# Turning B and x of a state-space layer by 32x32 blocks and DMAs instead of by TensorE transposes

## The chip, the cores and the metric

The kernel runs on one core of a Trainium2 chip. The metric is device time in microseconds (us) for one execution. TensorE (PE in the profile) does the matmuls, with its weight loads shown as PEld; VectorE is DVE, ScalarE is ACT, GpSimd is POOL; SyncE (SP) only issues DMAs here.

## The reference, cut to what matters

Two layers on 512 tokens of width 1024, with a residual around each: a state-space layer (a chunked scan) and a latent attention layer, then a final RMS norm. The change lies in the first layer, whose scan is, for one of 8 groups of 4 heads (64 wide), with the sequence cut in 4 chunks of 128 tokens:

```python
cb = einsum('bctgn,bcsgn->bgcts', cc, bc)                       # C B^T within a chunk
y_diag = einsum('bgcts,bgrcts,bcsgrp->bctgrp', cb, decay_in, xc)  # xc = x * dt
chunk_states = einsum('bctgn,bgrct,bctgrp->bcgrpn', bc, decay_to_end, xc)
y_off = einsum('bctgn,bcgrpn,bgrct->bctgrp', cc, entering, exp(a_cum))
y = y_diag + y_off + d_skip * xs                                # then gate, group norm, out projection
```

B, C, x and the gate z come out of one input projection of the layer, a convolution over 4 tokens and a SiLU.

## The kernel before

Activations lie transposed: 128 channels on the partitions, 512 tokens along the free axis. A projection is done in about fp32 precision with three fast matmuls per 128x128 block of weights: the weight and the input are each split into a high and a low part (`whi`, `wlo`, `ah`, `al`), by a ScalarE copy (L272) and a VectorE subtraction (L273). Each output block of 128 channels takes 24 matmuls of 512 columns (8 input blocks times 3, L291), in four lots of 6.

A loop over the 8 groups interleaves two things on TensorE. The feed is the input projection of the next group, `ssm_in(g + 1)`: six blocks B, C, x0, x1, z0, z1 of 24 matmuls, so 144 in all. The pieces are the steps of the scan of the present group, class `SSD`: `cb` (turn B with 3 transposes into PSUM, L71, copy it to `BT` by ScalarE, L73; 8 small matmuls C B^T, L77; mask it and multiply it into the four decay tiles L, L79 and L81), `x(0)` and `x(1)` (turn a pair of heads with 4 transposes, L89, then multiply by dt into `xdt`, L92, and by the decay to the chunk's end into `xw`, L94), `states` (3 matmuls of `BT` and `xw`, issued as 6, L105, and the scan over chunks, L109 to L113) and `y` (matmuls L130 and L138, then VectorE L144 to L148).

`sched` sets the order on TensorE by hand: each lot of 6 matmuls of the feed adds 1.296 to a counter, and a piece is put in when its due time is reached. The due times of groups 1 to 7 are `P1`: `cb` 1.0, `x(0)` 2.4, `x(1)` 3.8, `states` 12.0, `y` 18.2; so `cb` comes after 1 lot of the next projection, `x(0)` after 2, `x(1)` after 3, `states` after 10 and `y` after 15 of 24. The group norm of the group before (`GN`, 16.84) comes after 13 lots. In the last group the feed is the output projection instead, and its own group norm is due at `G7` = 33.0, after 26 lots. `mla` follows.

Only TensorE's order is written out. On the other engines and on the DMA queues the framework's scheduler places an instruction when its inputs are ready and nothing that stands earlier in the program wants the engine; each engine and queue then works through its list in that order.

SyncE's queue issues nearly all DMAs: the weights (`load_weight`, L263, two buffers `raw` of 128x1024 fp32), the decay rows `L` (L627, once the `yd` matmuls of the group before have freed their buffers) and the rows `E` (L123, L124). The last step of the first layer already turns a tensor by way of DRAM, once, for the residual: VectorE turns 32x32 blocks (L681), and four DMAs per tile write them to `hd` (L684) in runs of 32 values.

Of the kernel before, what the change touches and what calls it, by code (L numbers as in the profile page):

```python
# [10 lines left out]
F32 = mybir.dt.float32  # L11
# [4 lines left out]
P = 128  # L16
T = 512
D = 1024
KD = D // P
NCH = T // P  # L20
# [17 lines left out]
SU = (0.64, 1.42)  # L38
P0 = (6.0, 6.8, 11.91, 15.25, 17.25, 24.88, 34.5)
P1 = (1.0, 2.4, 3.8, 12.0, 18.2)  # L40
GN = 16.84
G7 = 33.0
SF = (0.02, 0.1, 2.1, 3.1)
# [11 lines left out]
class SSD:  # L55
# [8 lines left out]
    def cb(self):  # L64
        nc, net, wk, v = self.nc, self.net, self.wk, self.nc.vector
        B, C = self.st["B"], self.st["C"]
        ch = lambda ap: ap.rearrange("p (c s) -> p c s", c=NCH)
        pb = net.ssd_aux()
        for c in range(3):
            s = slice(c * P, (c + 1) * P)  # L70
            nc.tensor.transpose(pb[:, s], B[:, s], net.ident)  # L71
        self.BT = wk.tile([P, 3 * P], F32, tag="BT", name=net.nm("BT"), bufs=1)
        nc.scalar.copy(self.BT[:], pb[:, :3 * P])  # L73
        pc = net.ssd_aux()
        for c in range(NCH):
            s = slice(c * P, (c + 1) * P)
            nc.tensor.matmul(pc[:, s], B[:, s], C[:, s], start=True, stop=True)  # L77
        cb = wk.tile([P, T], F32, tag="cb", name=net.nm("cb"), bufs=2)
        v.tensor_tensor(ch(cb[:]), ch(pc[:]), net.triu[:, None, :].to_broadcast([P, NCH, P]), op=ALU.mult)  # L79
        for L in self.L:  # L80
            v.tensor_tensor(L[:], L[:], cb[:], op=ALU.mult)  # L81

    def x(self, j):
        nc, net, wk, v = self.nc, self.net, self.wk, self.nc.vector
        x = self.st[f"x{j}"]
        px = net.ssd_aux()
        for c in range(NCH):
            s = slice(c * P, (c + 1) * P)
            nc.tensor.transpose(px[:, s], x[:, s], net.ident)  # L89
        h0 = 4 * self.g + 2 * j  # L90
        xp = wk.tile([P, NCH, 2, 64], F32, tag="xdt", name=net.nm("xdt"), bufs=2)
        v.tensor_tensor(xp[:], px[:].rearrange("p (c h d) -> p c h d", c=NCH, h=2),  # L92
                        self.dt[:, :, h0:h0 + 2].unsqueeze(3).to_broadcast([P, NCH, 2, 64]), op=ALU.mult)
        v.tensor_tensor(self.xw[:, :, 2 * j:2 * j + 2, :], xp[:, :3],  # L94
                        self.dend[:, :3, h0:h0 + 2].unsqueeze(3).to_broadcast([P, 3, 2, 64]), op=ALU.mult)
        self.xdt.append(xp)
# [55 lines left out]
class Net:  # L152
# [8 lines left out]
    def build(self):  # L161
        tc, nc, ctx = self.tc, self.nc, self.ctx
        pool = lambda name, bufs, **k: ctx.enter_context(tc.tile_pool(name=name, bufs=bufs, **k))
        self.const = pool("const", 1)
        self.wraw = pool("wraw", 2)
        self.whi = pool("whi", 3)
        self.wlo = pool("wlo", 3)
        self.act = pool("act", 8)
        self.o16 = pool("o16", 16)
        self.nrm = pool("nrm", 1)  # L170
        self.res = pool("res", 8)
        self.dram = pool("dram", 1, space=bass.MemoryType.DRAM)

        const = self.const
        self.xs = []
        self.cols = const.tile([P, C_N], F32, name="cols")
        self.ident = const.tile([P, P], F32, name="ident")[:]
        self.rows = const.tile([P, 2 * NH], F32, name="rows")

        self.phase, self.group, self.before, self.head = "", [], [], None  # L180
        self.wq = []
        self.wpos = self.wload = 0
        self.wraws = []
        self.wready = {}
        for g in range(NG):
            for i in range(6):
                self.wq.append(("w", U_IN + 6 * g + i))
        for i in range(16):
            self.wq.append(("w", U_OUT0 + i))
        for i in range(6):  # L190
            self.wq.append(("w", U_M1 + i))
        self.wq += [("w", U_MZ + i) for i in range(3)] + [("ua", 0), ("w", U_MZ + 3), ("ub", 0), ("uc", 0), ("w", U_MZ + 4)]
        out = [("w", U_OUT1 + i) for i in range(16)]
        for h in range(14):
            j = h // 2 + 1
            self.wq += [("ua", j)] if h % 2 == 0 else [("ub", j), ("uc", j)]
            if h < 11:
                self.wq.append(("w", U_MZ + 5 + h))
            self.wq += [out.pop(0) for _ in range({11: 1, 12: 1, 13: 2}.get(h, 0))]
        self.wq += out  # L200

        with tc.tile_pool(name="ps_s", bufs=1, space=bass.MemoryType.PSUM) as ps, \
                tc.tile_pool(name="ssm", bufs=2) as wk:
            self.ps, self.wk = ps, wk
            self.ssm()
        with tc.tile_pool(name="ps_m", bufs=1, space=bass.MemoryType.PSUM, reuse_waits="tile") as ps, \
                tc.tile_pool(name="mla", bufs=2, reuse_waits="tile") as wk:
            self.ps, self.wk = ps, wk
            self.mla()
# [50 lines left out]
    def load_weight(self, kind, idx):  # L260
        n = {"w": 1024, "ua": 1024, "ub": 640, "uc": 512}[kind]
        raw = self.wraw.tile([P, n], F32, tag="raw", name=self.nm("raw"))
        self.nc.sync.dma_start(raw[:], self.t[kind][idx])  # L263
        return raw

    def split_weight(self, raw, cuts=()):
# [70 lines left out]
    def sumsq(self, tiles, n, pstag, pool=None, tags=("r0", "rt", "rr"), after=None):  # L337
        nc = self.nc
        acc = None
        for x in tiles:  # L340
            sq = self.nrm.tile([P, T], F32, tag="sq", name=self.nm("sq"), bufs=SQ)
            i = nc.scalar.activation(sq[:], x, AF.Square)
            if after is not None:
                self.link(i, [after])
            if acc is None:
                acc = self.nrm.tile([P, T], F32, tag="sqa", name=self.nm("sqa"))
                nc.vector.tensor_scalar(acc[:], sq[:], self.eps_of(n), None, op0=ALU.add)
            else:
                nc.vector.tensor_tensor(acc[:], acc[:], sq[:], op=ALU.add)
        pool = pool or self.nrm  # L350
        hi = pool.tile([P, T], F32R, tag=tags[0], name=self.nm("sqh"))
        lo = pool.tile([P, T], F32R, tag=tags[1], name=self.nm("sql"))
        nc.scalar.copy(hi[:], acc[:])
        nc.vector.tensor_tensor(lo[:], acc[:], hi[:].bitcast(F32), op=ALU.subtract)
        ps = self.ps.tile([P, T], F32, tag=pstag, name=self.nm("pssq"), bufs=self.bufs[pstag])
        nc.tensor.matmul(ps[:], self.onesr[:], hi[:], start=True, stop=False)
        nc.tensor.matmul(ps[:], self.onesr[:], lo[:], start=False, stop=True)
        return ps[:]

    def ssm(self):  # L360
        tc, nc, t, wk = self.tc, self.nc, self.t, self.wk
# [12 lines left out]
        for k in range(KD):  # L374
            x = self.res.tile([P, T], F32, tag="res", name=self.nm("x"))
            nc.sync.dma_start(x[:], t["x"][k])
            self.xs.append(x)
            if k % 2 == 0:
                s = slice(k * P, (k + 2) * P)
# [15 lines left out]
        for k in range(KD):  # L395
            a = self.o16.tile([P, T], F32R, tag="o", name=self.nm("vh"))
# [32 lines left out]
            ul.append(b)  # L429

        gn = []
        self.silus(0)
        for g in range(NG):
            ys, q = [], []
            pieces = [] if g == 0 else [(GN, late)]
            if g == 0:
                begin = lambda: q.append(SSD(self, 0, self.lexp(0), ys))
                pieces += [(SU[0] + SU[1] * k, scaled) for k in range(KD)]
                pieces += [(P0[0], step), (P0[1], step), (P0[1] + 0.1, begin)]
                at = P0[2:]  # L440
            else:
                q.append(SSD(self, g, self.lexp(g), ys))
                at = P1
            pieces += [(at[0], lambda: q[0].cb()), (at[1], lambda: q[0].x(0)), (at[2], lambda: q[0].x(1)),
                       (at[3], lambda: q[0].states()), (at[4], lambda: q[0].y())]
            if g + 1 < NG:
                mid = (vh, vl, lambda: r, MID) if g == 0 else (uh, ul, None, 0)
                self.sched(self.ssm_in(g + 1, uh, ul, mid), pieces)
                self.silus(g + 1)
                late = functools.partial(lambda g, ys: gn.extend(self.gnorm(g, ys)), g, ys)  # L450
            else:
                self.part = []
                pieces.append((G7, lambda: gn.extend(self.gnorm(g, ys))))
                self.sched(self.out_half(gn, 0, U_OUT0, [t["x"][k] for k in range(KD)]), pieces)
# [616 lines left out]
```

## Time and profile before

| | us |
|---|---|
| median of 3 runs (lowest to highest) | 837.02 (836.73 to 837.34) |
| the profiled execution | 836.13 |
| its span in the trace | 834.0 |

The difference of 2.1 us between the last two lies outside the span, at start and end. In the trace, the scan layer's groups 1 to 6 follow each other with one period: the matmuls after `yd` begin at 197.55, 237.67, 277.79 us and so on. The first layer ends at about 415 us. A row of the chain of waits gives the start, the length and the work that the end of the kernel waited for; in that chain a matmul counts from one start to the next, so 60 matmuls of 512 columns take 13.83 us, while the groups of instructions give each a longer, overlapping time.

### The profile page before, as it was taken

How to read it: one execution, taken by the hardware profiler on the slowest of the kernel's cores; microseconds unless marked ns; L12 is line 12 of the kernel's file. 1: busy time of each engine (PE TensorE's matmuls, PEld its weight loads, DVE VectorE, ACT ScalarE, POOL GpSimd, SP SyncE). 2: the span in 40 equal slices, each digit the busy share in tenths (PEclk: the TensorE clock that was granted, in tenths of full speed). 3: DMA queues.
4: the chain of work that ended last, by engine and by line, in shares of the span. 5: the costliest groups of instructions: out<-in, count | busy, mean ns of one | idle time of the engine just before them, and what ended most of it. 6: DMA issues, size and time to landing. Idle time of an engine off the chain costs nothing.

```text
span 834.0 us, 11549 instructions
## 1 busy us (share of the span) xinstructions
PE 819.3 (98%) x4228; PEld 691.8 (83%) x4228; DVE 644.9 (77%) x1234; ACT 450.4 (54%) x794; POOL 0.2 (0%) x4
## 2 busy tenths in 40 slices
PE   7999999999999999999999999999999999999996
PEld 5887888888888888888888888888888888888885
DVE  7999898979787989778566787786767869675544
ACT  7567755545465657434353654556547557554233
POOL 0000000000000000000000000000000000000000
PEclk9999999999999999999999999999999999999999
DMA  6364543423242423333555142222222224331212
GB/s 227 103 191 141 155 147 106 152 99 129 101 139 90 152 76 127 115 121 94 130 130 132 54 130 64 79 72 76 63 64 58 90 78 152 101 97 56 86 66 101
DMA packets 50856, 90.55 MB, mean 109 GB/s; under 512 B 21552, under 2 KB 23088, under 8 KB 50800
## 3 DMA queue, kind: packets, MB, share of 16 engines
q1 hardware_dynamic: 50080, 88.77, 34.0%
q10 hardware_dynamic: 720, 1.05, 0.3%
q8 instruction: 33, 0.54, 0.3%
q14 instruction: 23, 0.19, 0.1%
HBM read 83.12 MB, written 4.33 MB: 105 GB/s over the span
## 4 chain that ended last, share of the span: by engine, by line
PE 92%; DVE 3%; DMA 2%; ACT 1%; SPq 1%; issue 0%; DVEq 0%; ACTq 0%
PE mm L291 55%; PE ot L941 11%; PE s L793 5%; PE mm L300 4%; PE po L835 4%; PE mm L773 3%; PE pt L817 2%; PE yd L138 2%; PE yd L291 1%; PE aux L130 1%; PE aux L105 1%; DMA x<-in_x_dram 1%; PE aux L77 1%; PE aux L89 1%; DMA L<-ac_d 1%; DVE wlo L273 1%
## 5 line engine op out<-in xcount | busy, mean ns | idle before, releaser
L272 ACT CAST whi<-raw 128x1024 fp32r<-128x1024 f32 (+3 forms) x132 | 127.0, 965 | 210.3 <-PE mm L291 172.8
L273 DVE TENSOR_TENSOR wlo<-raw,whi 128x1024 fp32r<-128x1024 f32 (+3 forms) x132 | 146.8, 1115 | 54.6 <-ACT whi L272 54.3
L291 PE MATMUL mm<-ah,whi 128*128 128x512 f32 x384 | 154.0, 401 | 0.0
L291 PE MATMUL mm<-ah,wlo 128*128 128x512 f32 x384 | 150.3, 391 | 0.4 <-DVE wlo L273 0.4
L291 PE MATMUL mm<-al,whi 128*128 128x512 f32 x384 | 149.9, 390 | 0.0
L291 PE MATMUL mm<-vh,whi 128*128 128x512 f32 x224 | 89.4, 399 | 0.8 <-ACT whi L272 0.8
L291 PE MATMUL mm<-vh,wlo 128*128 128x512 f32 x224 | 87.9, 392 | 0.7 <-DVE wlo L273 0.7
L291 PE MATMUL mm<-vl,whi 128*128 128x512 f32 x224 | 87.6, 391 | 0.0
L291 PEld LDWEIGHTS mm<-ah,wlo 128*128 128x128 f32 x384 | 72.1, 188 | 16.1 <-DVE wlo L273 0.8
L291 PEld LDWEIGHTS mm<-ah,whi 128*128 128x128 f32 x384 | 72.2, 188 | 15.3 <-issue 1.4
L291 PEld LDWEIGHTS mm<-al,whi 128*128 128x128 f32 x384 | 72.2, 188 | 14.4 <-DVE al L312 0.3
L941 PE MATMUL ot<-whi,ah 128*128 128x512 f32 (+1 forms) x136 | 52.4, 385 | 0.0
L941 PE MATMUL ot<-whi,al 128*128 128x512 f32 (+1 forms) x136 | 51.5, 379 | 0.0
L941 PE MATMUL ot<-wlo,ah 128*128 128x512 f32 (+1 forms) x136 | 51.4, 378 | 0.0
L291 PEld LDWEIGHTS mm<-vh,wlo 128*128 128x128 f32 x224 | 42.1, 188 | 10.7 <-DVE wlo L273 1.5
L291 PEld LDWEIGHTS mm<-vh,whi 128*128 128x128 f32 x224 | 42.2, 188 | 9.4 <-ACT whi L272 1.1
L223 ACT ACTIVATE p<-p,st 128x128 f32<-128x128 f32 (+1 forms) x64 | 36.1, 564 | 25.3 <-DVE st L805 25.2
L291 PEld LDWEIGHTS mm<-vl,whi 128*128 128x128 f32 x224 | 42.2, 188 | 7.3
L821 ACT CAST ph<-pt 128x512 fp32r<-128x512 f32 (+1 forms) x64 | 26.4, 421 | 33.3 <-PE pt L817 32.8
L291 PE MATMUL mm<-ch,whi 128*128 128x512 f32 x104 | 42.6, 410 | 0.0
L291 PE MATMUL mm<-ch,wlo 128*128 128x512 f32 x104 | 40.9, 393 | 0.0
L291 PE MATMUL mm<-cl,whi 128*128 128x512 f32 x104 | 40.8, 392 | 0.0
(223 smaller groups left out, 1637.7 us busy)
## 6 DMA issues: line engine op xcount, KB each, us to landing
raw<-in_w_dram SPq DMA_DIRECT2D x100, 512.0 KB, 3.3
L<-ac_d SPq DMA_DIRECT2D x32, 256.0 KB, 3.9
E<-ea_d SPq DMA_DIRECT2D x32, 128.0 KB, 3.5
raw<-in_ua_dram SPq DMA_DIRECT2D x8, 512.0 KB, 3.3
raw<-in_ub_dram SPq DMA_DIRECT2D x8, 320.0 KB, 2.8
x<-in_x_dram SPq DMA_DIRECT2D x8, 256.0 KB, 4.4
res<-in_x_dram SPq DMA_DIRECT2D x8, 256.0 KB, 3.1
hd<-ht SPq DMA_DIRECT2D x32, 64.0 KB, 3.5
```

The source lines that it names most:

```text
L138: nc.tensor.matmul(yd[64 * h:64 * h + 64, s], self.xdt[j][:, c, h, :], self.L[2 * j + h][:, s], start=True, stop=True)
L223: i = self.nc.scalar.activation(out, in_, func, **k)
L272: nc.scalar.copy(hi[:, a:b], raw[:, a:b])
L273: nc.vector.tensor_tensor(lo[:, a:b], raw[:, a:b], hi[:, a:b].bitcast(F32), op=ALU.subtract)
L291: self.nc.tensor.matmul(ps, a, b, start=i == 0, stop=i == len(seq) - 1)
L300: self.nc.tensor.matmul(p, seq[i][0], seq[i][1], start=i == 0, stop=i == 3 * ks - 1)
L773: nc.tensor.matmul(ps[:, c2 * 256:(c2 + 1) * 256], a, b, start=i == 0, stop=i == 5)
L793: nc.tensor.matmul(ps[:, :n], x[:, s], y[:, :n], start=k == 0, stop=k == 4)
L817: nc.tensor.transpose(pt[:, (b - kb) * P:(b - kb + 1) * P], probs[h][b][:, kb * P:(kb + 1) * P], self.ident)
L821: nc.scalar.copy(ph[:, :n], pt[:, :n])
L835: nc.tensor.matmul(po[:, kb * P:], x, y, start=kb == 0 and k == 0, stop=kb == NCH - 1 and k == 2)
L941: nc.tensor.matmul(ps[:, a:b], x, y, start=start and i == 0, stop=stop and i == 5)
```

## The change

For groups 2 to 7 (`FLIP = 2`) the 3 transposes of B and the 8 of x leave TensorE. In their place stand two new pieces. `flip` turns x0, x1 and B by VectorE in 32x32 blocks into tiles `tp`, and writes each with 4 DMAs of 64 KB into one of two DRAM tensors, so that the turned tensor lies there by rows. `back` reads x0 and x1 (256 KB each, runs of 512 bytes) into the `xdt` tiles and B (192 KB) into `BT`. `x(j)` then multiplies the loaded tile by dt in place. The due times of these groups are `P2`: `flip` 0.2, `cb` 1.0, `back` 8.0, `x(0)` 11.5, `x(1)` 11.6, `states` 15.5, `y` 21.0. From group 0's pieces on, all weights of both layers go over GpSimd's queue instead of SyncE's.

```diff
+P2 = (0.2, 1.0, 8.0, 11.5, 11.6, 15.5, 21.0)
+FLIP = 2
...
     def cb(self):
...
-        pb = net.ssd_aux()
-        for c in range(3):
-            s = slice(c * P, (c + 1) * P)
-            nc.tensor.transpose(pb[:, s], B[:, s], net.ident)
-        self.BT = wk.tile([P, 3 * P], F32, tag="BT", name=net.nm("BT"), bufs=1)
-        nc.scalar.copy(self.BT[:], pb[:, :3 * P])
+        if self.g < FLIP:
+            pb = net.ssd_aux()
+            for c in range(3):
+                s = slice(c * P, (c + 1) * P)
+                nc.tensor.transpose(pb[:, s], B[:, s], net.ident)
+            self.BT = wk.tile([P, 3 * P], F32, tag="BT", name=net.nm("BT"), bufs=1)
+            nc.scalar.copy(self.BT[:], pb[:, :3 * P])
...
+    def flip(self):
+        nc, net, wk = self.nc, self.net, self.wk
+        d = net.flip_d[self.g % 2]
+        turned = d[:].rearrange("(j a) n -> a j n", a=32)
+        for m, name in enumerate(("x0", "x1", "B")):
+            t = wk.tile([P, T], F32, tag="u", name=net.nm("tp"), bufs=3)
+            nc.vector.transpose(t[:], self.st[name][:])
+            for i in range(4):
+                n = m * P + 32 * i
+                nc.sync.dma_start(turned[:, :, n:n + 32], t[32 * i:32 * i + 32, :].rearrange("a (j n) -> a j n", n=32))
+
+    def back(self):
+        nc, net, wk = self.nc, self.net, self.wk
+        rows = net.flip_d[self.g % 2][:].rearrange("(c p) n -> p c n", p=P)
+        self.px = []
+        for j in range(2):
+            xp = wk.tile([P, NCH, 2, 64], F32, tag="xdt", name=net.nm("xdt"), bufs=2)
+            nc.sync.dma_start(xp[:].rearrange("p c h d -> p c (h d)"), rows[:, :, j * P:(j + 1) * P])
+            self.px.append(xp)
+        self.BT = wk.tile([P, 3 * P], F32, tag="BT", name=net.nm("BT"), bufs=1)
+        nc.sync.dma_start(self.BT[:].rearrange("p (c n) -> p c n", c=3), rows[:, :3, 2 * P:])
...
     def x(self, j):
...
+        if self.g < FLIP:
+            px = net.ssd_aux()
+            for c in range(NCH):
+                s = slice(c * P, (c + 1) * P)
+                nc.tensor.transpose(px[:, s], x[:, s], net.ident)
+            px = px[:].rearrange("p (c h d) -> p c h d", c=NCH, h=2)
+            xp = wk.tile([P, NCH, 2, 64], F32, tag="xdt", name=net.nm("xdt"), bufs=2)
+        else:
+            xp = self.px[j]
+            px = xp[:]
+        v.tensor_tensor(xp[:], px,
                         self.dt[:, :, h0:h0 + 2].unsqueeze(3).to_broadcast([P, NCH, 2, 64]), op=ALU.mult)
...
     def load_weight(self, kind, idx):
...
-        self.nc.sync.dma_start(raw[:], self.t[kind][idx])
+        self.wqueue.dma_start(raw[:], self.t[kind][idx])
...
+        self.flip_d = [self.dram.tile([T, 3 * P], F32, name=f"flip{i}") for i in range(2)]
...
-                at = P1
+                at = P1 if g < FLIP else (P2[1],) + P2[3:]
+                if g >= FLIP:
+                    pieces += [(P2[0], lambda: q[0].flip()), (P2[2], lambda: q[0].back())]
...
+            self.wqueue = nc.gpsimd
```

More of the change, by code (lines that the diff above doesn't have):

```diff
@@ L85, in x @@
         x = self.st[f"x{j}"]
[L86 to L89, printed above, removed]
         h0 = 4 * self.g + 2 * j
-        xp = wk.tile([P, NCH, 2, 64], F32, tag="xdt", name=net.nm("xdt"), bufs=2)
-        v.tensor_tensor(xp[:], px[:].rearrange("p (c h d) -> p c h d", c=NCH, h=2),
+        if self.g < FLIP:
[9 more added lines that the diff above has]
+        v.tensor_tensor(xp[:], px,
                         self.dt[:, :, h0:h0 + 2].unsqueeze(3).to_broadcast([P, NCH, 2, 64]), op=ALU.mult)
@@ L180, in build @@
         self.phase, self.group, self.before, self.head = "", [], [], None
+        self.wqueue = nc.sync
         self.wq = []
```

## The prediction

> **What bounds the kernel now.** I read first the head of the page with the chain of waits by engine, then the busy time by stretch, then the chain through one group.
>
> ```profile
> span 834.0 us, 11549 instructions
> PE 819.3 (98%) x4228; PEld 691.8 (83%) x4228; DVE 644.9 (77%) x1234; ACT 450.4 (54%) x794; POOL 0.2 (0%) x4
> PE 92%; DVE 3%; DMA 2%; ACT 1%; SPq 1%; issue 0%; DVEq 0%; ACTq 0%
> ```
>
> ```profile
> core 0: us, PE busy (x) PEld busy (x) DVE busy (x) ACT busy (x) POOL busy (x), PEclk, DMA share, GB/s
> 197.55:209.18 11.63, 11.63 (x52) 9.61 (x53) 11.60 (x26) 6.52 (x12) 0.00 (x0) 1.00 0.56 184
> 197.55:237.67 40.12, 40.12 (x216) 33.67 (x216) 34.16 (x61) 22.32 (x34) 0.00 (x0) 1.00 0.35 118
> 97.00:137.20 40.20, 40.20 (x217) 33.76 (x216) 38.98 (x73) 26.61 (x43) 0.00 (x0) 1.00 0.41 128
> 52.00:97.00 45.00, 44.00 (x248) 36.57 (x248) 39.74 (x66) 32.99 (x61) 0.00 (x0) 1.00 0.60 186
> ```
>
> TensorE sets the end. From 197.55 to 237.67 us (one group) it is busy for all of 40.12 us at full granted clock, so what leaves its list there shortens the group, if nothing that it needs comes late. VectorE is second: 34.16 of 40.12 us, 85%, and without a gap in the first 11.6 us. The chain through that group:
>
> ```profile
> 197.55 13.83 PE mm L291 x60
> 211.38 0.33 PE aux L71 x3
> 211.71 0.89 PE aux L77 x8
> 212.60 1.39 PE mm L291 x6
> 214.00 0.43 PE aux L89 x4
> 214.43 1.39 PE mm L291 x6
> 215.82 0.44 PE aux L89 x4
> 216.26 9.56 PE mm L291 x42
> 225.82 1.30 PE aux L105 x6
> 234.43 1.34 PE aux L130 x12
> 235.77 1.90 PE yd L138 x32
> 237.67 2.50 PE mm L291 x10
> ```
>
> The whole chain is TensorE's, and the eleven transposes (L71, L89) are links of it.
>
> **What leaves TensorE.** In the chain they take 0.33 + 0.43 + 0.44 = 1.20 us. Each x piece also cuts the feed: a lot of 6 matmuls between pieces takes 1.39 us, against 6 x 9.56/42 = 1.37 in the long run, so two cuts less give some 0.05. That is 1.25 us a group, and 6 x 1.25 = **7.5 us**. The BT copy (L73) leaves ScalarE, which has 22.32 of 40.12 us to do and so gives no time back.
>
> [...]
>
> **What VectorE gets.**
>
> ```profile
> L681 DVE STREAM_TRANSPOSE ht<-res x8: 699/711/712, 388.2 to 431.6; 128x512 f32<-128x512 f32 x8
> L684 SPq DMA_DIRECT2D hd<-ht x32: 341/487/856, 389.0 to 448.9; - x32
> DMA to landing us min/median/max: 2.3/3.4/3.8
> L92 DVE TENSOR_TENSOR xdt<-aux,dt 128x512 f32<-128x512 f32 x16 | 10.3, 684 | 0.0
> L94 DVE TENSOR_TENSOR xw<-xdt,dec 128x384 f32<-128x384 f32 x16 | 8.3, 551 | 0.0
> ```
>
> The first two rows are this same step in another place (times in ns as min/median/max). Three transposes of 0.711 us add 2.13 us a group. L92 reads SBUF in place of PSUM; L94 has two SBUF inputs already, 0.551 us for 384 columns or 1.43 ns a column, where L92 has 0.684 for 512, 1.34 ns, so I leave it at 0.684. VectorE then has 34.16 + 2.13 = 36.3 us in a group of 38.9, or 93%. What hides this is that VectorE is not in the chain; the stretch from 97.00 shows how far that goes: VectorE at 38.98 of 40.20 us, 97%, and TensorE still busy throughout. So nothing for it.
>
> **The way of x through DRAM.** It has a deadline, and this is where the change is decided. I count from T0, the end of the `yd` matmuls of the group before (197.55 us in the chain above).
>
> The deadline: `states` now comes after 12 lots in place of 10. From T0 there are 42 matmuls left of the old feed (`y` sits after 17 lots, 102 of 144), 6 of the new one, 0.89 us of L77, then 66 more. At 13.83/60 = 0.2305 us each, 114 matmuls are 26.3, so T0 + 27.2.
>
> When x1 is ready: before, its 24th matmul is the 6th after T0. Now `y` comes two lots later, so it lies 6 matmuls ahead of `y`: 1.39 + 1.34 + 1.90 = 4.63 us before T0, a shift of 6.0 us.
>
> ```profile
> 205.82 0.64 ACT L232 ACTIVATE x<-x 128x512 f32<-128x512 f32 x1
> ...
> 209.83 1.05 ACT L272 CAST whi<-raw 128x1024 fp32r<-128x1024 f32 x1 [2.86 <-PE mm L291]
> ```
>
> ```profile
> 202.04 1.22 DVE L273 TENSOR_TENSOR wlo<-raw,whi 128x1024 fp32r<-128x1024 f32 x1
> ...
> 204.68 2.24 DVE L634 TENSOR_SCALAR L<-L,ac 128x128 f32<-128x128 f32 x11
> ...
> 208.49 0.69 DVE L349 TENSOR_TENSOR sqa<-sqa,sq 128x512 f32<-128x512 f32 x1
> ```
>
> Its SiLU ended at 206.46, T0 + 8.9, so now near T0 + 2.9. The first gap of VectorE came at 209.18, T0 + 11.6.
>
> No row shows this round trip, so I bound it. The reads' nearest rows are those of `hr` and, slower, of `L`; `raw` serves for the weights further on:
>
> ```profile
> hr<-hd SPq DMA_DIRECT2D x8, 256.0 KB, 2.9
> L<-ac_d SPq DMA_DIRECT2D x32, 256.0 KB, 3.9
> raw<-in_w_dram SPq DMA_DIRECT2D x100, 512.0 KB, 3.3
> ...
> L923 SPq DMA_DIRECT2D hr<-hd x8: 319/320/332, 691.5 to 704.1; - x8
> ```
>
> - Early end: transpose done at T0 + 3.6; 4 issues of 0.49 us, landing 3.4 later, T0 + 9.0; three reads issued in 1.0 and landed 2.9 later, T0 + 12.9; L92 and L94 for both pairs 2 x (0.68 + 0.55) = 2.5, so T0 + 15.4. That is 11.8 us early.
> - Late end: all three transposes wait for the gap, T0 + 13.7; 4 issues of 0.86 and a landing of 3.8, T0 + 20.9; reads 1.0 + 3.9, T0 + 25.8; VectorE 2.5, T0 + 28.3. That is 1.1 us too late in each group.
>
> So the stall is 0 at the one end and 6 x 1.1 = 6.6 us at the other; below nothing it cannot be. I take 0: the middle, T0 + 21.8, is 5.4 us early, and in VectorE's first 11.6 us other work of the next feed (L273, L634 above) is already taken in between the steps of `y`, so a transpose can be too. x0 and B are ready earlier than x1.
>
> **SyncE's queue.** It gets 12 x 0.49 + 3 x 0.32 = 6.8 us of issues a group and loses six weights. Behind a `back` that waits for the last write stand only `L` and `E` rows, for `y` at the end of the group (their buffers come free after T0 in both versions); with the weights gone nothing that TensorE needs sooner is held up. If the weights had stayed, they would stand behind that wait.
>
> **Weights on GpSimd's queue.** No DMA in this trace comes from there. The nearest row is SyncE's: landing after 3.3 us at the median. How much later may they be? The buffer freed by the subtraction at 202.04 (ended 203.26) is used by the ScalarE copy at 209.83: 6.6 us. That copy waits for TensorE to release a `whi` (its row says so); three lie in turn, so its own first matmul is 48 matmuls, some 11 us, later, 2.3 of which go to copy and subtraction. The cover is 6.6 - 3.3 + 8.7 = 12 us a weight; if it were gone, each further us of delay would cost one on TensorE per weight. Both bounds (as fast, or twice 3.3) give nothing. A gain is bounded by the idle time of TensorE while groups 0 and 1 start, when weights do queue behind other issues: 45.00 - 44.00 = 1.0 us. I take 0.
>
> [...]
>
> **The end of the layer.** `y` of group 7 moves two lots nearer to its group norm.
>
> ```profile
> 356.30 1.90 PE yd L138 x32
> 365.87 0.68 DVE L354 TENSOR_TENSOR sql<-sqa,sqh 128x512 fp32r<-128x512 f32 x1
> 373.39 0.23 PE pssq L356
> ```
>
> Before, the norm's inputs were ready at 366.55, 8.4 us after `yd`; TensorE asks for them after 9 lots now, 54 x 0.23 = 12.4 us. Covered.
>
> **Sum.** 836.13 - 7.5 = 828.6 us for the profiled execution. That execution lies 0.9 us under the median of 837.02, so the forecast is **829.5 us**.
>
> **Rivals.**
>
> 1. *Nearly hidden or nearly lost: the late end above.* TensorE waits at `states` for `xw` some 1.1 us a group: 829.5 + 6.6 = 836.1. For it: VectorE's full 11.6 us after T0. Against: x1's shift of 6.0 us. About no change.
>
> 2. *The round trip becomes the bound.* VectorE keeps the transposes behind its backlog and all 12 writes queue behind them: T0 + 13.7; twelve issues of about 0.6 us (between the median 0.49 and the longest 0.86) are 7.2; landing 3.8, T0 + 24.7; reads 1.0 + 3.9, VectorE 2.5, T0 + 32.1. That is 4.9 us late, 29.4 over six groups: 859 us. It is slower from the point where the wait exceeds 1.25 us a group. For it: SyncE issues one DMA after another, and VectorE, in order, may stand at L92 with a weight's subtraction behind it. Against: x0 and B need not wait for x1, and 8 of 12 issues can go first.
>
> [...]
>
> **How the numbers follow.** Forecast (no stall beyond 0.3 us a group, 828 to 831.5): 0.62. Part of the gain eaten, 831.5 to 835.3: 0.07. Rival 1: 0.09. Rival 2: 0.19, half of it under 840 since its wait can be anything past its point. Rival 3: 0.03. The measurement can tell about 0.2%, 1.7 us, from no change, so faster is 0.62 + 0.07 less a remainder = 0.68, same 0.10, slower 0.22. The forecast's own range is 828 to 831.5; the lower end takes 1.0 us of start-up gain and half a us for the run. To leave out no more than 2 in 10 the upper end goes to 840.
>
> **What would show it.** Right: the period between `yd` ends falls from 40.12 to about 38.9 us in six groups; L71 counts 6 and L89 16; VectorE near 93% there; no wait at L105. Wrong: TensorE waiting at L105 for L94, or L94's line behind a DMA of `xdt` (rivals 1 and 2); ScalarE's L272 behind `raw` and TensorE behind L272 (rival 3); or a period that shrinks by less with no wait in it, so that the transposes cost less than their links.

## The result, and the profile after

The changed kernel takes 849.33 us (848.52 to 853.25) against 836.94 (836.73 to 837.34): a ratio of 1.0159, 95% interval 1.0135 to 1.0184. It is **slower by 12.4 us**, where 7.5 us less were forecast. The profiled execution of it took 848.52 us, with a span of 846.4 us against 834.0. One execution of experiment 3 below ran at a granted clock of 0.70 and took 1115 us; it is left out of that experiment's time.

The head of its page (busy time by engine, then the chain by engine):

```profile
span 846.4 us, 11624 instructions
PE 817.7 (97%) x4162; PEld 687.7 (81%) x4162; DVE 655.0 (77%) x1252; ACT 448.3 (53%) x788; POOL 63.4 (7%) x122
PE 88%; DVE 5%; DMA 2%; ACT 2%; issue 2%; SPq 1%; DVEq 0%; ACTq 0%
```

TensorE has its 66 matmul instructions less (4228 to 4162, eleven for each of six groups), and the chain is no longer its alone: 88% where it was 92%, and 2% "issue", time in which the engine stands still and the profile shows nothing that it waits for. Where this happens shows in the chain from the `yd` matmuls of one group to those of the next. First the chain in the first group that is turned, group 2, and in the last, then the busy time by stretch:

```profile
148.19 6.57 issue
154.76 2.90 PE aux L135 x6
157.65 2.56 PE mm L322 x6
...
167.53 1.90 PE yd L168 x32
...
355.23 3.29 issue
358.51 2.90 PE aux L135 x6
```

```profile
core 0: us, PE busy (x) PEld busy (x) DVE busy (x) ACT busy (x) POOL busy (x), PEclk, DMA share, GB/s
118.49:169.43 50.94, 44.36 (x217) 36.60 (x217) 41.98 (x72) 23.97 (x35) 3.71 (x7) 0.93 0.48 127
154.76:160.20 5.44, 5.44 (x13) 4.32 (x14) 2.13 (x5) 0.00 (x0) 0.00 (x0) 0.51 0.00 0
208.48:247.77 39.29, 39.09 (x205) 32.50 (x205) 35.76 (x65) 22.06 (x33) 3.18 (x6) 1.00 0.58 159
326.37:372.09 45.72, 41.12 (x205) 33.51 (x205) 37.41 (x68) 20.16 (x32) 3.81 (x7) 0.96 0.52 153
```

In group 2 `states` (L135, once L105) waits 6.57 us, and then TensorE runs at a granted clock of 0.51 for the next 5.44 us: L135 takes 2.90 us where it took 1.30, the next lot 2.56 where it takes 1.39. So the stall costs 6.57 + 1.60 + 1.17 = 9.3 us. The third row is a later group: 39.29 us, near the forecast. The fourth is the last group, with TensorE idle for 45.72 - 41.12 = 4.6 us, 3.29 of them at `states` (the last rows of the chain above).

Laid side by side, from one end of `yd` to the next (us):

| | before | after | difference |
|---|---|---|---|
| start to the end of group 1's `yd` | 117.31 | 118.49 | +1.2 |
| group 2 | 40.12 | 50.94 | +10.8 |
| group 3 | 40.12 | 39.05 | -1.1 |
| groups 4 to 6, each | 40.12 | 39.30 | -0.8 |
| group 7 | 40.29 | 45.72 | +5.4 |
| from there to the end | 475.8 | 474.3 | -1.5 |

Of group 2's 10.8 us, some 2.7 are only moved: its `y` and those behind it stand two lots later than group 1's, and the last row gives this back. Without that, group 2 loses 8.1 us and the part behind the scan 1.2.

What `states` waits for in group 2 is `xw`: the profile names nothing, but the last L124 ends at 154.66 us and L135 starts at 154.76. VectorE's own order of work there (start, length; idle time before it in brackets), and SyncE's:

```profile
131.15 1.30 DVE L92 STREAM_TRANSPOSE tp<-x 128x512 f32<-128x512 f32 x2
132.37 0.68 DVE L92 STREAM_TRANSPOSE tp<-B 128x512 f32<-128x512 f32 x1
...
149.07 1.23 DVE L304 TENSOR_TENSOR wlo<-raw,whi 128x1024 fp32r<-128x1024 f32 x1 [1.98 <-ACT whi L303]
150.21 2.31 DVE L645 SCALAR_TENSOR_TENSOR x<-mm,cols,x 128x511 f32<-128x511 f32 x3
152.43 1.28 DVE L122 TENSOR_TENSOR xdt<-xdt,dt 128x512 f32<-128x512 f32 x2
153.64 1.02 DVE L124 TENSOR_TENSOR xw<-xdt,dec 128x384 f32<-128x384 f32 x2
```

```profile
131.89 8.40 SPq L95 DMA_DIRECT2D flip<-tp  x12
140.33 1.05 SPq L103 DMA_DIRECT2D xdt<-flip  x2
```

```profile
L103 SPq DMA_DIRECT2D xdt<-flip x2: 457/473/489, 140.3 to 140.9; - x2
DMA to landing us min/median/max: 5.2/5.3/5.3
```

The reads of x start at 140.3 and 140.9 us and land 5.2 to 5.3 us after their start, so by 146.2 us (B's, started at 142.1, lands after 4.7 us, by 146.8); yet the multiply by dt (L122) starts at 152.43. In between VectorE ends the convolution of C at 147.1, is *idle* for 1.98 us, then subtracts a weight (L304) and runs the convolution of the feed's third block (L645). Its list has them in this order, and both hang on matmuls that TensorE issues just ahead of `states`. TensorE waits for VectorE, which had been waiting for TensorE. With the data there at 146.2 and 2.3 us of multiplies, the landing alone would by these rows have cost an estimated 0.3 us after 148.19, where TensorE stops; the experiments had to show whether that holds.

### The profile page after: what moved, and what is told of

It is laid out like the page before. It is cut to its first block, busy times and chain, and to the rows that moved or that the text cites. A ratio compares the mean times of both kernels' runs of the same rounds, so it can differ in the third digit from the quotient of the medians.

```text
span 846.4 us, 11624 instructions
## 1 busy us (share of the span) xinstructions
PE 817.7 (97%) x4162; PEld 687.7 (81%) x4162; DVE 655.0 (77%) x1252; ACT 448.3 (53%) x788; POOL 63.4 (7%) x122
## 4 chain that ended last, share of the span: by engine, by line
PE 88%; DVE 5%; DMA 2%; ACT 2%; issue 2%; SPq 1%; DVEq 0%; ACTq 0%
PE mm L322 52%; PE ot L976 10%; PE s L828 5%; PE mm L331 4%; PE po L870 3%; PE mm L808 3%; PE pt L852 2%; PE yd L168 2%; PE aux L135 2%; PE yd L322 1%; PE aux L160 1%; DMA x<-in_x_dram 1%; DVE wlo L304 1%; PE aux L80 1%; ACT whi L303 1%
## 5 line engine op out<-in xcount | busy, mean ns | idle before, releaser
L304 DVE TENSOR_TENSOR wlo<-raw,whi 128x1024 fp32r<-128x1024 f32 (+3 forms) x132 | 146.6, 1115 | 49.5 <-ACT whi L303 49.2
L294 POOL DMA_DIRECT2D raw<-in_w_dram x94 | 50.3, 535 | 621.4 <-DVE wlo L304 376.6
```

Source lines behind the costliest of these rows:

```text
L294: self.wqueue.dma_start(raw[:], self.t[kind][idx])
L304: nc.vector.tensor_tensor(lo[:, a:b], raw[:, a:b], hi[:, a:b].bitcast(F32), op=ALU.subtract)
```

## The experiments

The two theories throughout: **order**, that L122 and L124 stand too late in VectorE's list; **data**, that the turned tiles come back too late. Beside them, the queue of the weights. Each diff is against the changed kernel unless it says otherwise.

**1. The weights alone** (`e1_weights_only`). No group is turned.

```diff
-FLIP = 2
+FLIP = 8
```

> All groups keep the TensorE transposes and the old due times; only the weights go over GpSimd's queue. Theory (two single stalls): the loss of the changed kernel comes from waits at states in groups 2 and 7, and the weights' queue costs only what the two traces show at the start of the scan (1.2 us) and behind the first rope exchange of the second layer (1.3 us): 837.0 + 2.5 = 839.5 us. Rival (the weights are the loss): 845 us or more. Rival of the prediction (the queue is free): 837.

Measured: 838.65 us, ratio 1.0026 (1.0016 to 1.0036). All groups keep 40.12 us (the last 40.29). So GpSimd's queue costs the groups nothing while TensorE transposes, and about 2 us in all, at the start (group 0's `yd` ends at 90.89 us, before at 89.44) and in the second layer. There the transfers that swap rows for the rotation (`rsw`) land up to 4.0 us after their issue, before 2.2 at most, and a weight's first matmul waits 0.9 us for its subtraction instead of 0.2.

**2. The weights in the groups alone** (`e8_weights_in_groups`): the kernel before, with GpSimd's queue only while groups 1 to 6 run.

```diff
-FLIP = 2
+FLIP = 8
...
-            self.wqueue = nc.gpsimd
+            self.wqueue = nc.gpsimd if 0 < g < NG - 1 else nc.sync
```

> The kernel before with the weights on GpSimd's queue only while groups 1 to 6 run. Theory: the 2.0 us of e1 come from the start of the scan and from the second layer, where a weight and a small transfer on the path are now in flight together: 837 within 0.6. Rival (each weight costs a little): 838 or more.

Measured: 836.74 us, ratio 0.9994 (0.9984 to 1.0003). No cost is left, which puts that of experiment 1 outside groups 1 to 6.

**3. The turning alone** (`e2_turn_only`), with all weights on SyncE.

```diff
-            self.wqueue = nc.gpsimd
```

> The turning by VectorE and DRAM as in the changed kernel, the weights on SyncE's queue as before. Theory (two single stalls): the 2.5 us of the weights' queue come back and the stalls stay: about 847 us. Rival (the weights had to move): they stand behind the reads that wait for the writes, TensorE waits for weights in each group: well above 849. Rival (the weights are the loss): 837 or less.

Measured: 857.12 us (856.71 to 859.70), ratio 1.0254 (1.0236 to 1.0273), where 847 were expected. The stall now comes in groups 2, 4 and 6, with the same length each time in the chain:

```profile
147.78 5.64 issue
...
233.88 5.64 issue
239.52 2.90 PE aux L135 x6
...
319.61 5.64 issue
```

Three waits of 5.64 us, to the hundredth, are not what data coming late would look like. VectorE's list in group 4:

```profile
234.71 2.32 DVE L644 SCALAR_TENSOR_TENSOR x<-mm,cols,x 128x511 f32<-128x511 f32 x3 [3.12 <-ACT x L642]
236.95 0.68 DVE L122 TENSOR_TENSOR xdt<-xdt,dt 128x512 f32<-128x512 f32 x1
```

It idles 3.12 us for the third block's convolution and only then runs L122, though x had landed by 228.3 us and B by 231.2, before `states` was due at 233.88. The time is that of the rival on the weights, its mechanism is not: from 90 to 400 us ScalarE waits for a weight's DMA once, for 0.6 us. What the queue changed is VectorE's list, in which the stall stands in three of groups 2 to 6 instead of one.

**4. Other groups** (`e3_groups_3_to_6`): only groups 3 to 6 are turned.

```diff
-FLIP = 2
+FLIP = (3, 4, 5, 6)
...
-        if self.g < FLIP:
+        if self.g not in FLIP:
```

> As the changed kernel, but groups 2 and 7 keep the TensorE transposes and the old due times. Theory (two single stalls): groups 3 to 6 give 1.1 + 3 x 0.8 = 3.5 us, the weights' queue takes 2.5: 837.0 - 1.0 = 836 us, no wait over 0.3 us at states. Rival (the first group that turns always stalls, whichever it is): group 3 now loses what group 2 lost, some 10.8 us: 847.

Measured: 846.58 us, ratio 1.0114 (1.0098 to 1.0131); the rival held. The stall moved to group 3, now the first turned one: 6.56 us, then L135 in 2.90 again. So with the weights on GpSimd's queue it belongs to the first turned group, whichever that is. What is special about it is the group ahead, whose `y` still comes after 15 lots instead of 17. And the data are not late here: x had landed by 186.3 us and B by 188.7, 3.0 us before `states` was due at 191.74, and the stall is the same.

**5. The due times alone** (`e4_due_times`): the kernel before, with TensorE's transposes, on the later due times.

```diff
+P2 = (1.0, 11.5, 11.6, 15.5, 21.0)
...
-                at = P1
+                at = P1 if g < 2 else P2
```

> The kernel before with only the later due times in groups 2 to 7 (x at 11.5 and 11.6, states at 15.5, y at 21.0); transposes on TensorE, weights on SyncE. Theory: the due times by themselves move nothing, 837 us within 0.5. Rival (y later delays what follows it): part of the loss shows here, 839 or more.

Measured: 839.28 us, ratio 1.0034 (1.0021 to 1.0048); the rival held. Groups 3 to 6 take 40.46 us each, 0.34 more, without any turning through DRAM, and the last 41.56 against 40.29. In the chain of such a group the weight's subtraction, the steps of C's convolution and L93 and L95 (the multiplies) follow each other up to `states`:

```profile
183.81 1.23 DVE wlo L274
185.03 0.66 DVE C L611
185.69 0.60 DVE xdt L93
186.29 0.66 DVE C L611
...
189.41 1.53 PE aux L106 x6
```

Moving `x` and `states` this close together has a price by itself: VectorE gets to `xw` among the feed's own work.

**6. The convolution moved behind `xw`** (`e5_order`). A link makes the third block's convolution (in the last group its addition) wait in VectorE's list behind `xw`; nothing else moves.

```diff
-        v.tensor_tensor(self.xw[:, :, 2 * j:2 * j + 2, :], xp[:, :3],
+        net.turned = v.tensor_tensor(self.xw[:, :, 2 * j:2 * j + 2, :], xp[:, :3],
...
+            if half == 0 and m == 2:
+                self.link(e, [self.turned])
...
+                if i == 2 and g > FLIP:
+                    self.link(e, [self.turned])
```

> The changed kernel with one thing more: VectorE takes x(0) and x(1) of a turning group ahead of its work on the third block of the feed (the convolution of x0, or in group 7 the residual's addition). That block is the one whose last matmul stands right before states. Theory (VectorE's order): xw stands behind work that TensorE only releases when it has come to states, so the wait there is as long as that work, 6.6 us in groups 2 and 3.3 in 7; put ahead, the waits fall to 1.5 us or less, and with them the time at the lower clock: 849.3 - 8 - 4 = about 838 us. Rival (the data are late): the reads land only then, the waits stay within 2 us of what they were: 845 or more.

Measured: 848.26 us, ratio 1.0142 (1.0125 to 1.0158): the number of the data theory. VectorE's list in group 2 says why it doesn't settle it:

```profile
149.90 1.23 DVE L304 TENSOR_TENSOR wlo<-raw,whi 128x1024 fp32r<-128x1024 f32 x1 [1.98 <-ACT whi L303]
151.04 0.68 DVE L122 TENSOR_TENSOR xdt<-xdt,dt 128x512 f32<-128x512 f32 x1
...
152.96 0.56 DVE L124 TENSOR_TENSOR xw<-xdt,dec 128x384 f32<-128x384 f32 x1
153.43 2.31 DVE L647 SCALAR_TENSOR_TENSOR x<-mm,cols,x 128x511 f32<-128x511 f32 x3
```

The convolution went behind (153.43) and the stall fell by 1.98 us, from 6.57 to 4.59, near the 2.31 that it takes; the weight's subtraction still stood ahead, with VectorE idle before it.

**7. The subtractions moved too** (`e9_order_all`): as experiment 6, and the subtractions of the weights of the feed's next two blocks stand behind `xw` as well.

```diff
+            self.wlo_op = nc.vector.tensor_tensor(lo[:, a:b], raw[:, a:b], hi[:, a:b].bitcast(F32), op=ALU.subtract)
...
+            if half == 0 and m in (3, 4):
+                self.link(self.wlo_op, [self.turned])
...
+            if g > FLIP and i in (3, 4):
+                self.link(self.wlo_op, [self.turned])
```

> The changed kernel, with VectorE's order corrected fully: in groups 2 to 7 the convolution (or residual add) of the feed's third block and also the weight subtractions of the feed's next two blocks stand behind the four multiplies that make xdt and xw; due times and queues as changed. Theory (the place of the dt multiplies in VectorE's list makes the stall): in the first turning group the stall at states falls from 6.57 us to 1.5 or less, what the round trip itself leaves; the last group's 3 us shrink as well; 838 to 843 us in all. Rival (the data come back late, the place only hid it): the stall stays at 4 us or more and the time at 846 or above, as with the convolution alone moved.

Measured: 840.12 us, ratio 1.0038 (1.0023 to 1.0053). The chain through group 2, and the part of VectorE's list there that ends with L122:

```profile
150.08 0.93 issue
151.00 1.53 PE aux L135 x6
...
190.06 1.29 PE aux L135 x6
```

```profile
146.20 2.32 DVE L651 SCALAR_TENSOR_TENSOR C<-mm,cols,C 128x511 f32<-128x511 f32 x3 [2.33 <-ACT C L649]
148.43 0.68 DVE L122 TENSOR_TENSOR xdt<-xdt,dt 128x512 f32<-128x512 f32 x1
```

The stall is 0.93 us with the same due times, the same transfers and the same queues: **5.6 of the 6.57 us were the order**. What is left is mostly order too, some 0.6 us of it: x had landed by 147.8 us, but L122 stood behind the convolution of C until 148.43. Groups 3 to 6 go from 39.3 (39.05 in group 3) to between 38.84 and 38.90 us. What stays slower than before is the last group (43.80 us) and the start and second layer.

**8. `y` of group 1 later** (`e6_y1_late`). No link; `y` of the two groups that aren't turned gets the due time 21.0.

```diff
-                at = P1 if g < FLIP else (P2[1],) + P2[3:]
+                at = P1[:4] + P2[6:] if g < FLIP else (P2[1],) + P2[3:]
```

> The changed kernel, but y of groups 0 and 1 is due at 21.0 too, so that x1 of the next group leaves TensorE ahead of y already for group 2. Theory: group 2 then is like groups 3 to 6, its stall of 6.6 us and the slow matmuls after it are gone, group 7 is not touched: 849.3 - 8.3 = 841 us. Rival (the first group that goes through DRAM stalls whatever its due times): 849.

Measured: 842.43 us, ratio 1.0061 (1.0041 to 1.0081). Group 2 takes 39.30 us, as the others, with 0.19 us of wait. The last group was expected to stay as it was and has 47.78 us, 2.1 more than after the change. With group 1's `y` at 17 lots x0 is turned ahead of the end of `yd`, and VectorE's list comes out in another order by itself.

**9. `states` one lot later** (`e11_states_late`).

```diff
-P2 = (0.2, 1.0, 8.0, 11.5, 11.6, 15.5, 21.0)
+P2 = (0.2, 1.0, 8.0, 11.5, 11.6, 16.5, 21.0)
```

> The changed kernel with one number changed: states due at 16.5, one lot of 6 matmuls later. If the stall is a fixed point in VectorE's list that TensorE reaches too early, it shrinks by one lot, 1.37 us, in groups 2 and 7, and the 0.4 us per group in groups 3 to 6 go: 844 to 845 us. If the stall moves along with the order (what stands ahead of the multiply is released by the matmuls ahead of states, whatever their number), it stays near 6.6 us: 847 or above.

Measured: 847.27 us, ratio 1.0129 (1.0105 to 1.0153). The time is the rival's, the stall the theory's: in group 2 it is 5.23 us, shorter by 1.34, one lot, and groups 3 to 6 take 38.82. But the last group takes 46.74, a microsecond more, which was not expected.

**10. Three parts together** (`e7_all_three`): the links of experiment 6, the two due times, and GpSimd's queue only while groups 1 to 6 run.

```diff
-P2 = (0.2, 1.0, 8.0, 11.5, 11.6, 15.5, 21.0)
+P2 = (0.2, 1.0, 8.0, 11.5, 11.6, 16.5, 21.0)
...
+                at = P1[:4] + P2[6:] if g < FLIP else (P2[1],) + P2[3:]
...
-            self.wqueue = nc.gpsimd
+            self.wqueue = nc.gpsimd if 0 < g < NG - 1 else nc.sync
```

> The order of e5, the due time of y of e6, states one lot later (16.5), and GpSimd's queue for the weights only while groups 1 to 6 run. Theory: no wait over 0.3 us at states in any of the six groups, each of them 1.1 to 1.25 us shorter than before: 837.0 - 7 = 830 us. Rival (group 7 has another cause): 833 to 836.

Measured: **830.06 us** (829.72 to 831.82), ratio 0.9923 (0.9908 to 0.9938). It beats both kernels, and one group in the busy time by stretch is TensorE's alone again (the row below). The gain is that of five groups, 1.30 us each; the last group, 40.22 us, gains next to nothing against its 40.29, where 1.1 or more were expected:

```profile
159.24:198.06 38.82, 38.82 (x206) 32.59 (x205) 35.51 (x65) 22.14 (x33) 3.16 (x6) 1.00 0.60 161
```

**11. The same without the links** (`e10_due_and_queue`), the diff against experiment 10.

```diff
-            if half == 0 and m == 2:
-                self.link(e, [self.turned])
...
-                if i == 2 and g > FLIP:
-                    self.link(e, [self.turned])
```

> The three-part version (y of group 1 at 21.0, states one lot later at 16.5, weights on GpSimd's queue only while groups 1 to 6 run) without the links that put the feed's third block behind xw. If the due times alone give the turned data their time: 830 to 831 us, like the version with the links, and no stall at states. Rival (the order on VectorE also has to be set by hand): 833 us or more, with a wait at states in at least the last group.

Measured: 830.93 us, ratio 0.9931 (0.9914 to 0.9948). The groups take 38.82 us without a link; only the last, 41.13 us, shows a wait, 0.66 us. So the due times do nearly all of it: with them, the scheduler's own order costs 0.9 us.

**12. The same with the queue as changed** (`e12_queue_throughout`): experiment 10, but the weights go over GpSimd's queue from group 0 to the end; the diff is against experiment 10.

```diff
-            self.wqueue = nc.gpsimd if 0 < g < NG - 1 else nc.sync
+            self.wqueue = nc.gpsimd
```

> The three-part version with one thing undone: the weights stay on GpSimd's queue from group 0 to the end, as in the change. The two runs on weights alone put that at about 2 us, in the start and in the second layer: 832 us here, against 830 with the queue used in groups 1 to 6 only. Rival (those 2 us are hidden when the scan is shorter): 830 to 831.

Measured: 838.69 us, ratio 1.0015 (0.9999 to 1.0031). Both expectations fell: the queue costs 8.6 us here, not 2. Of the spans' difference, 8.7 us, the last group holds 6.3 (46.55 against 40.22 us) and the start 2.3. The second layer differs by 0.1. Of the 6.3, 3.49 are the wait at `states` and some 1.8 the lower clock behind it (a mean of 0.89 from 347.6 to 363.41 us, against 1.00 from 342.66 to 354.79 in experiment 10; from L135 to `y` it takes 9.09 us against 7.24). ScalarE and VectorE in the last group, and the chain:

```profile
347.48 1.04 ACT L303 CAST whi<-raw 128x1024 fp32r<-128x1024 f32 x1 [2.93 <-DMA raw<-in_w_dram]
```

```profile
348.56 1.23 DVE L304 TENSOR_TENSOR wlo<-raw,whi 128x1024 fp32r<-128x1024 f32 x1 [2.75 <-ACT whi L303]
349.70 0.68 DVE L122 TENSOR_TENSOR xdt<-xdt,dt 128x512 f32<-128x512 f32 x1
```

```profile
347.59 3.49 issue
351.08 1.67 PE aux L135 x6
```

Here a weight does come late: ScalarE waits 2.93 us for its DMA, VectorE, in order, for ScalarE, and L122 stands behind. The line of that DMA and the one of `con`, the second layer's 768 KB of constants on SyncE's queue, in this kernel and in experiment 10 (the first row of each pair: issues and their first start; the second: landing):

```profile
L294 POOL DMA_DIRECT2D raw<-in_w_dram x4: 527/529/692, 339.0 to 350.1; - x4
...
DMA to landing us min/median/max: 3.5/4.0/7.3
```

```profile
L695 SPq DMA_DIRECT2D con<-in_con_dram x1: 485/485/485, 339.3 to 339.3; - x1
```

```profile
L695 SPq DMA_DIRECT2D con<-in_con_dram x1: 427/427/427, 353.1 to 353.1; - x1
```

With the weights on SyncE's queue, `con` stands behind them and starts at 353.1 us. With the weights gone from there it starts at 339.3, between two weights, and one of the four weights in that stretch lands after 7.3 us instead of 4.0. The changed kernel shows the same: `con` starts at 347.7, between weights issued at 347.4 and 348.5, and the second of these lands after 7.0 us. That `con` is what delays it is argued from these rows; it wasn't moved alone. In experiment 1 `con` also starts early (335.2 us) and the last group loses nothing: with TensorE's transposes, due after 2 and 3 lots, `xw` is made long before these weights.

## Why the prediction was wrong

**The step that failed is "I take 0"** in the round trip: the belief that VectorE would run L92 and L94 (now L122, L124) once their data lay there. In the group from 208.48 us x1 was back at T0 + 19.4, inside the bounds of T0 + 12.9 and T0 + 25.8, and L122 took it up 6.3 us later. In group 2 x was back at T0 + 27.7, later than the late end but before the deadline there, and L122 took it up 6.2 us later. Rival 2 named that VectorE "may stand at L92 with a weight's subtraction behind it"; it was the other way round, L92 behind the subtraction, and its price (4.9 us in each of six groups, 859 us) was that of late data. What came of this step was 9.3 us in one group. The 6.7 us in the last (its 5.4 and the 1.25 not gained) belong mainly to a second step that failed, **the "I take 0" for the weights on GpSimd's queue**: with the later due times and the links, that queue alone makes 6.3 us of difference in the last group (experiment 12).

- *Transposes off TensorE, 1.25 us a group*: right. With no wait left the period is 38.82 against 40.12, so 1.30 us (experiment 10). TensorE's transposes are as cheap as the chain before had them: 1.30/11 = 0.12 us each by this, 1.20/11 = 0.11 there.
- *VectorE's 2.13 us more, "nothing"*: right as load. It is busy for 35.8 of 39.29 us in the group of the third row above, below the 36.3 worked out. But a share of busy time says nothing of the order in the list, and the order was the cost.
- *The deadline, T0 + 27.2*: right for groups 3 to 6 (in the group from 208.48, `states` is due at 235.47, T0 + 27.0). For group 2 it was T0 + 29.7, and *x1's shift of 6.0 us* does not hold there: group 1's `y` stays after 15 lots. The prediction gave all six groups the shift. The transposes came at T0 + 12.7, as in the late end (T0 + 13.7 for their end), and the 12 writes behind them took 8.40 us to issue, 0.70 each against the 0.49 and 0.86 taken. The data of x were back by T0 + 27.7 and VectorE, busy with C's convolution, free at T0 + 28.6, so with 2.3 us of multiplies 1.2 us were late; the 0.93 of experiment 7 fits that remainder.
- *"so a transpose can be too"*: half right. In groups 3 to 6 x0 is turned before T0, but x1 and B only behind the backlog of `y` and the `L` rows, at T0 + 8.8. `xw` came just in time, behind C's convolution, where 5.4 us were expected to be spare:

```profile
217.32 0.71 DVE L92 STREAM_TRANSPOSE tp<-x 128x512 f32<-128x512 f32 x1
...
232.05 2.31 DVE L645 SCALAR_TENSOR_TENSOR C<-mm,cols,C 128x511 f32<-128x511 f32 x3
234.28 0.68 DVE L122 TENSOR_TENSOR xdt<-xdt,dt 128x512 f32<-128x512 f32 x1
235.00 0.56 DVE L124 TENSOR_TENSOR xw<-xdt,dec 128x384 f32<-128x384 f32 x1
```

  The wait of 0.19 us and 1.53 instead of 1.30 for L135 are the 0.4 us by which these groups miss 38.82. The due times bring a like loss without any DMA (0.34, experiment 5); the prediction had not priced them at all.
- *Weights on GpSimd's queue, 0*: wrong, and the largest miss beside the order. Alone it is about 2 us; together with the turning, 8.6 (experiment 12), and the rows of experiment 12 show why: the cover of 12 us a weight counted for TensorE's matmuls and not for what stands behind the weight in VectorE's list. Of the signs listed for weights that come late (rival 3) one appeared, ScalarE's copy behind `raw` (1.53 and 2.60 us in the last group of the changed kernel). But GpSimd's issues keep to 0.53 us at the median, follow the subtraction that frees their buffer by some 0.3 us there, and the weights land after 3.7 us at the median against 3.3.
- *SyncE's queue, 0; the end of the layer, covered*: nothing in the trace speaks against either, but for the early `con`, a transfer that moved *up* since the weights left. The prediction looked only for what might move down.

The runs split the loss in two: from 849.33 us, the due times and links bring 10.6 (to 838.69), and confining GpSimd's queue to groups 1 to 6 another 8.6 (to 830.06). With both, the kernel lies 0.6 us above the forecast of 829.5; that is partly luck, since it has other due times and another use of the queue, and its gain comes from five groups and not six. What stays open: the start (the end of group 0's `yd` lies at 89.2 to 94.0 us in the versions, 89.44 before), for which no single cause was found; and why the last group is longest in experiments 8 and 9. In experiment 7, whose last group has no wait at `states` and still takes 43.80 us, the chain runs through a transfer of the `L` rows of 8.02 us, and ScalarE waits 2.43 us for a weight; neither was tested alone.

## What to carry to other kernels

When work leaves the bound engine for one that runs its list in order, ask what will stand ahead of it there and which of that hangs on the bound engine itself: here such a loop stalled both, with VectorE busy for 41.98 of group 2's 50.94 us. Check the first and the last round of a loop apart from the steady ones; here both large losses lay there, and the four rounds between behaved nearly as forecast. And moving a stream to another queue also lets what stood behind it go earlier, as `con` did here (at 339.3 us instead of 353.1).

## What the hardware showed that was not expected

- A stall cost more than its length here. After 6.57 us without a matmul the granted clock was 0.51 for 5.44 us, some 2.8 us more; after 0.93 us of wait (experiment 7) L135 took 1.53 us, hardly more than 1.30. Shorter waits did it too: after 3.29 us in the changed kernel's last group the granted clock was 0.50 for 2.90 us, and after 3.04 us in experiment 6's L135 took 2.90 us again.
- Twelve writes of 64 KB in runs of 32 values took 0.70 us each to issue from SyncE when they came in one row (8.40 us), against 0.49 at the median for the same kind of write in the trace before. In group 4 of experiment 3, with the weights on SyncE, twelve in a row took 0.57 each; what makes the difference was not tested.
- The wait was 6.57 us after the change and 6.56 in another group of experiment 4, and 5.64 three times in experiment 3. Waits that agree so closely pointed to a fixed order ahead of any reading of the list.
